# Hybrid decoder layer, first block: when the feed-forward weights are rounded, where a low half is made, and the order of loads around the output projection

## Chip, cores and metric

The kernel runs on one core of a Trainium2 chip. The metric is the device time of one execution in microseconds (us). The kernel before took 2597.31 us (median of three runs, 2594.66 to 2601.35).

## What is computed

One layer of a decoder on a prompt (2048 rows of 1024) and on a small sample group (8 x 4 rows): RMSNorm, one combined input projection, dilated windowed attention in 8 heads beside a spatial gating unit, one output projection with a residual add, RMSNorm, a SwiGLU feed-forward (width 2816) with a residual add, a last RMSNorm. The caches are written out as well. All arrays are float32. The change concerns the end of the layer:

```python
    x = x + jnp.concatenate([att, u * gate], axis=-1) @ w_out
    x = x + _swiglu(x, norm2_g, w_gate, w_up, w_down)
    ...
def _swiglu(x, g, w_gate, w_up, w_down):
    h = _rmsnorm(x, g)
    return (jax.nn.silu(h @ w_gate) * (h @ w_up)) @ w_down
```

## The kernel before

**Arithmetic.** TensorE (PE) multiplies operands that are cut into a rounded high half, made on ScalarE (ACT), and the rest, a low half, made by a subtraction on GpSimd (POOL) or VectorE (DVE). A product is then three matmuls: high x high, high x low, low x high. `split_sb` does both halves: high on ACT (L135), low on POOL or on the engine given as `eng_lo` (L138). The gate and up products of a slice of 128 feed-forward columns are formed by a scheme with seven products in place of eight (q = 0 to 6, each of 12 matmuls in L1663 to L1665), whose weight operands are sums of the loaded quarters.

**Blocks.** The 16 row tiles of 128 go through the output projection and the feed-forward in three blocks: six, six and four tiles. The change lies in the first block, from about 940 to 1495 us.

**Output projection, first block.** Each tile has an open half (columns 0 to 511) and a second half. The open half of tile 0 is multiplied during the attention. Then come the open halves of tiles 1 to 5 (24 matmuls each, L1411 to L1413), then the second halves of tiles 0 to 5. The input of a tile is loaded with `load_cat` (L1390) from the tensor `cat_d` in memory and split with `split_cat` (L1399 to L1403). `B.banks = (2, 0, 3, 4, 5, 2)`: tile 5's open half uses the PSUM bank of tile 0's, so it waits until `first_half(0)` has added tile 0's open half to `acc` (`open_end`, DVE, L1422). The weights of the second half are loaded by `half1_load` (L1363, into the eight buffers `fr`) and split by `half1_split`. In the same stretch `factors` loads the last head's softmax factors (`zn` and `raw` from `f_d`, L1077), and `rest` merges them on POOL (L1084 to L1088), stores the result (L1106) and loads the last gain. `sources` loads the first gate and up quarters into `fr` as they come free (L1560).

In the second phase `norm2_slot` runs between the tiles: it adds the second half (L1422), squares (L1450), forms the root and scales on ACT (L1462, `pair`), and PE transposes the result two tiles later (L1474). In the same steps the operands of slice 0 are formed: scaled on POOL (L1569), summed on DVE (L1584 to L1593).

**Feed-forward, first block.** Slices f = 0 to 21. Slice 0 is cut in two parts (four and two tiles). The operands of slice f + 1 are made during slice f, one stage per product, from the tables `ODD_STAGES` and `EVEN_STAGES`; the quarters of slice f + 2 are scaled on ACT (`gained`, L1572, eight operations of 128 columns per stage) and partly summed by the tables `..._AHEAD`. `sums` runs on POOL (L1584, L1587, L1590, and L1593 for operand 5, which overwrites operand 1); `both_halves` rounds on ACT (L1600) and makes the low half on POOL (L1604); `keep` stores an operand for the later blocks (`ab_d`, L1596). Product q = 0 is copied out of PSUM by ACT (L1673), and DVE adds the next products to that copy (L1675, L1677, L1687 and so on). The products use four PSUM banks in turn. `roll` copies 512 KB of cache from memory to memory (L1308). `w_down` is loaded into the one buffer `fd` (L1643) and split by `split_down` into `dw`, in even slices behind q = 6 and in odd ones behind q = 3. The down products of a pair of slices run in the even slice behind products 3, 4 and 5, two tiles each (L1743); they use two PSUM banks, which DVE frees by adding them to `acc` (L1745).

**What sets the order.** Each engine works through its own queue in order. DMAs are issued by SyncE (SP) in order as well. `tick()` counts a step per half unit or product, and `later(n, ...)` places work n steps on; inside a step the order of the calls is the order in the queues.

Of the kernel before, what the change touches and what calls it, by code (L numbers as in the profile page):

```python
# [23 lines left out]
KD = D // P  # L24
# [41 lines left out]
def hymba_step(ctx: ExitStack, tc: tile.TileContext, A: dict, O: dict):  # L66
    nc = tc.nc
    sync, act, dve, pool, pe = nc.sync, nc.scalar, nc.vector, nc.gpsimd, nc.tensor
# [633 lines left out]
    for half in range(2):  # L702
        for ki, kind in enumerate(ORDER[half]):
            for gi, tiles in enumerate(GROUPS):
# [13 lines left out]
                for j, tj in enumerate(tiles):  # L718
# [23 lines left out]
                    else:  # L742
                        layer_norm(e + 1, t, lambda t=t: zn["g", t], P)

                        f = e + 4 + (3 if tj in (4, 5) else 0)
# [526 lines left out]
    FC = 2  # L1272
# [333 lines left out]
    def both_halves(f, j):  # L1606
# [9 lines left out]
    ODD_STAGES = (((sums, 4), (sums, 3), (keep, 0)), ((sums, 1), (both_halves, 0), (keep, 6), (keep, 2)), ((both_halves, 1), (keep, 4)),  # L1616
                  ((both_halves, 2), (keep, 3)), ((both_halves, 3), (keep, 1)), ((sums, 5), (both_halves, 4)), ((both_halves, 5),),
                  ((both_halves, 6), (keep, 5)), ())
    EVEN_STAGES = (((both_halves, 0), (keep, 3)), ((both_halves, 1), (keep, 1)), ((both_halves, 2),), ((both_halves, 3),),
                   ((sums, 5), (both_halves, 4)), ((both_halves, 5),), ((both_halves, 6), (keep, 5)), (), ())  # L1620
    ODD_AHEAD = {5: ((gained, 0), (gained, 1)), 6: ((gained, 2), (gained, 3))}
    EVEN_AHEAD = {3: ((gained, 0), (gained, 1)), 4: ((gained, 2), (gained, 3), (keep, 0)), 5: ((sums, 4), (sums, 3), (keep, 6)),
                  6: ((sums, 1), (keep, 2), (keep, 4))}
# [20 lines left out]

    wd = {}

    def split_down(f):
        wd[f % FC] = ob_pair("dw")
        split_sb(*wd[f % FC], raws.pop(("d", f)))

    def product(B, u, q):

# [262 lines left out]
    def first_block(B):  # L1915

        for i in (1, 2):
            load_cat(B, i, 0, KD, acc_place(2 * i))
        plan.run(10 ** 9)
        split_cat(B, 1)  # L1920
        split_cat(B, 2)
        B.place()
        load_cat(B, 3, 0, KD)
        merge_store(h - 1, 2, 4)
        merge_store(h, 1, 2)
        load_acc(B, 1)
        load_acc(B, 0)
        half1_load(*range(4))
        load_cat(B, 4, 0, KD)

        def factors():
            for ch in (2, 3):
                merge_load(h, ch)
            load_cat(B, 5, 0, KD)
            half1_load(*range(4, KD))

        def rest():
            for ch in (2, 3):
                merge(h, ch, pool)
            merge_store(h, 2, 4)  # L1940
            sync.dma_start(gain[0], dap(A["final_g"], 0, [[0, P], [1, D]]))

        def first_half(i):
            open_end(B, i)
            norm2_half(B, i, B.X[0][:, i, 0:512])

        def root_ahead():
            t_ = fl.tile([P, 4], F32, name="s1", tag="s1", bufs=6)
            act.activation(t_[:, 0:1], ident[:, 0:1], AF.Sqrt)

        w = last_half["w"]
        for n, what in ((1, [(w.turn, lambda: ps_t(1)), (w.store, zn_tile)]), (2, [(split_cat, B, 3), (factors,)]),
                        (4, [(split_cat, B, 4), (rest,)]), (5, [(half1_split, B, dve, 0, 1)]),
                        (6, [(split_cat, B, 5), (first_half, 0)]), (7, [(first_half, 1), (half1_split, B, dve, 2, 3), (sources, B, 0, 0, 1, 2, 3)]),
                        (8, [(half1_split, B, None, 4, 5)]), (9, [(half1_split, B, dve, 6, 7)]),
                        (10, [(root_ahead,), (sources, B, 1, 0, 1, 2, 3), (first_operands, B)])):
            later(n, both, *what)
        for i in (1, 2):
            open_unit(B, i)
        for i in (3, 4, 5):  # L1960
            open_unit(B, i)

        def more_acc(i):
            if i in (1, 2):
                load_acc(B, 2 * i)
                load_acc(B, 2 * i + 1)

        second_phase(B, range(6), more_acc)
# [38 lines left out]
    for bi, B in enumerate(blocks):  # L2007
# [13 lines left out]
        def one(u, q):  # L2021
# [25 lines left out]
                roll(1)  # L2047

            if f % 2 == 0 and q == 6:
                split_down(f)  # L2050
                load_down(f + 1)
            elif f % 2 == 1 and q == 3:
                split_down(f)
                if f + 1 < NF:
                    load_down(f + 1)
# [143 lines left out]
```

## Time and profile before

| | |
|---|---|
| median of three runs | 2597.31 us |
| profiled execution, its own time | 2594.14 us |
| its span (first to last instruction) | 2592.3 us |
| mean granted clock of PE | 0.985 |
| PE busy | 2467.8 us (95%) |
| PE weight loads busy | 2175.4 us (84%) |
| DVE / ACT / POOL busy | 1430.4 / 1221.5 / 1369.7 us |

Times in the views are us from the start of the span. A row of the timeline has start, duration, engine, line, operation, output<-inputs, shapes, count, and in brackets how long the engine stood idle before it and who released it. A row of the list of waits has the waiting engine and line, the releaser, then the total in us, how often, and the longest. A row of the windows has the stretch, its length, for each of PE, PE's weight loads, DVE, ACT and POOL the busy time (and the number of instructions), then PE's granted clock, the DMA share and GB/s. A row of the chain has start, duration and what it is.

### The profile page before, as it was taken

To read this page: it belongs to the slowest core of one execution; us is meant where nothing else is said; L and a number is where in the kernel's file an instruction comes from. 1 tells how busy PE (TensorE), PEld (TensorE's weight loads), DVE (VectorE), ACT (ScalarE), POOL (GpSimd) and SP (SyncE) were. 2 spreads that over 40 slices of the span, in tenths; PEclk is the share of its full clock that TensorE was granted. 3 is DMA by queue.
4 is the path that set the end of the run, shared out by engine and by line. 5 is a ranking of instruction groups with operands and counts; after the bars stand their busy time and mean duration, and the time that the engine had idled before them with its cause. 6 is when DMAs were issued, how large, how long until landed. Compare 5 with 4: busy or idle time off the path is not lost.

```text
span 2592.3 us, 38968 instructions
## 1 busy us (share of the span) xinstructions
PE 2467.8 (95%) x13598; PEld 2175.4 (84%) x13598; DVE 1430.4 (55%) x2783; ACT 1221.5 (47%) x2578; POOL 1369.7 (53%) x1068
## 2 busy tenths in 40 slices
PE   8998899999999889999999999999999999999996
PEld 6777776677988768898999988999999987999996
DVE  3359686345888877344444466544444457544445
ACT  5423335446878745554454545432332336444332
POOL 2035654123576745776776743554453634766662
PEclk9999999999999999999999999999999999999998
DMA  7764853588678674464564564455463643755553
GB/s 236 226 204 150 272 159 117 180 247 276 195 223 219 175 210 150 143 206 156 163 195 134 183 187 159 171 187 175 151 215 126 210 154 127 239 194 196 195 195 109
DMA packets 313409, 480.00 MB, mean 185 GB/s; under 512 B 25841, under 2 KB 178834, under 8 KB 307326
## 3 DMA queue, kind: packets, MB, share of 16 engines
q1 hardware_dynamic: 307740, 468.48, 56.7%
q10 hardware_dynamic: 5474, 9.04, 1.3%
q8 instruction: 108, 1.77, 0.3%
q14 instruction: 87, 0.71, 0.1%
HBM read 381.72 MB, written 165.83 MB: 211 GB/s over the span
## 4 chain that ended last, share of the span: by engine, by line
PE 36%; issue 8%; POOL 8%; DMA 4%; ACT 2%; DVE 2%; SPq 1%; POOLq 0%; ACTq 0%; DVEq 0%
PE ps_o L1743 12%; PE ps_m L1665 8%; PE ps_m L1663 8%; PE ps_m L1664 8%; POOL op L1604 2%; DMA ab_d<-pair 2%; ACT fr L1572 1%; POOL pair L1584 1%; POOL dw L138 1%; POOL fr L1587 1%; POOL pair L1593 1%; POOL pair L1590 1%; DMA out_yp_dram<-acc 1%; SPq L1390 1%; PE ps_o L1411 0%
## 5 line engine op out<-in xcount | busy, mean ns | idle before, releaser
L1604 POOL TENSOR_TENSOR op<-fr,op 128x512 fp32r<-128x512 f32 x385 | 488.6, 1298 | 285.1 <-ACT op L1600 273.9
L1665 PE MATMUL ps_m<-xh,op 128*128 128x384 f32 (+5 forms) x1932 | 610.8, 316 | 2.0 <-POOL op L1604 2.0
L1663 PE MATMUL ps_m<-xh,op 128*128 128x384 f32 (+5 forms) x1932 | 610.9, 316 | 0.0
L1664 PE MATMUL ps_m<-xl,op 128*128 128x384 f32 (+5 forms) x1932 | 609.8, 316 | 0.0
L1743 PE MATMUL ps_o<-dw,hw 128*128 128x512 f32 x2040 | 485.8, 393 | 14.8 <-DVE acc L1745 14.8
L1743 PEld LDWEIGHTS ps_o<-dw,hw 128*128 128x128 f32 x2040 | 380.5, 188 | 98.4 <-DVE acc L1745 21.9
L1663 PEld LDWEIGHTS ps_m<-xh,op 128*128 128x128 f32 x1932 | 364.2, 189 | 4.0
L1664 PEld LDWEIGHTS ps_m<-xl,op 128*128 128x128 f32 x1932 | 364.2, 189 | 3.5
L1665 PEld LDWEIGHTS ps_m<-xh,op 128*128 128x128 f32 x1932 | 364.1, 188 | 2.5 <-POOL op L1604 2.5
L1745 DVE TENSOR_TENSOR acc<-acc,ps_o 128x512 f32<-128x512 f32 (+1 forms) x362 | 247.1, 687 | 214.8 <-PE ps_o L1743 214.7
L1710 ACT ACTIVATE ps_t<-zn 128x384 f32<-128x384 f32 (+1 forms) x126 | 58.2, 462 | 463.9 <-DVE zn L1693 364.5
L1600 ACT ACTIVATE op<-fr 128x512 fp32r<-128x512 f32 x396 | 235.5, 623 | 20.8 <-DMA fr<-ab_d 18.1
L138 POOL TENSOR_TENSOR dw<-fd,dw 128x1024 fp32r<-128x1024 f32 x66 | 158.5, 2402 | 120.1 <-ACT dw L135 119.4
L318 PE MATMUL ps_s<-wh,xh 128*128 128x512 f32 x480 | 197.2, 411 | 6.1 <-ACT xh L135 6.0
L319 PE MATMUL ps_s<-wl,xh 128*128 128x512 f32 x480 | 191.7, 399 | 2.0 <-DVE wl L226 2.0
L320 PE MATMUL ps_s<-wh,xl 128*128 128x512 f32 x480 | 191.5, 399 | 0.0
L1604 POOL TENSOR_TENSOR op<-pair,op 128x512 fp32r<-128x512 f32 x63 | 81.2, 1297 | 117.1 <-ACT op L1600 117.1
L1720 ACT ACTIVATE hw<-ps_t 128x384 fp32r<-128x384 f32 (+1 forms) x126 | 56.1, 453 | 175.1 <-DVE ps_t L1716 174.1
L318 PEld LDWEIGHTS ps_s<-wh,xh 128*128 128x128 f32 x480 | 92.5, 193 | 35.9 <-issue 8.4
L319 PEld LDWEIGHTS ps_s<-wl,xh 128*128 128x128 f32 x480 | 92.8, 193 | 20.8 <-DVE wl L226 3.6
L320 PEld LDWEIGHTS ps_s<-wh,xl 128*128 128x128 f32 x480 | 92.2, 192 | 20.4 <-DVE xl L138 0.2
L135 ACT ACTIVATE dw<-fd 128x1024 fp32r<-128x1024 f32 x66 | 69.8, 1057 | 73.1 <-DMA fd<-in_w_down_dram 73.1
(489 smaller groups left out, 4769.6 us busy)
## 6 DMA issues: line engine op xcount, KB each, us to landing
fr<-ab_d SPq DMA_DIRECT2D x308, 256.0 KB
fd<-in_w_down_dram SPq DMA_DIRECT2D x66, 512.0 KB
out_ks_dram<-in_cache_k_dram SPq DMA_DIRECT2D x56, 512.0 KB
out_vs_dram<-in_cache_v_dram SPq DMA_DIRECT2D x56, 512.0 KB
ab_d<-fr SPq DMA_DIRECT2D x88, 256.0 KB
raw<-in_w_in_dram SPq DMA_DIRECT2D x72, 256.0 KB
qk_d<-pair SPq DMA_DIRECT2D x64, 256.0 KB
ab_d<-pair SPq DMA_DIRECT2D x63, 256.0 KB
```

Source lines behind the costliest of these rows:

```text
L135: act.activation(hi, src, AF.Copy)
L138: (eng_lo or pool).tensor_sub(lo, src, hi.bitcast(F32))
L318: pe.matmul(o[j], xh[:, k, :], wh, start=(k == 0), stop=False)
L319: pe.matmul(o[j], xh[:, k, :], wl, start=False, stop=False)
L320: pe.matmul(o[j], xl[:, k, :], wh, start=False, stop=(k == KD - 1))
L1600: act.activation(ops[f, j][0], ab[f][j], AF.Copy)
L1604: (pool if f or j in POOL_LOW else dve).tensor_sub(lo_, ab[f][j], hi.bitcast(F32))
L1663: pe.matmul(out, wh[:, ks], xh[:, :, k], start=(k == 0), stop=False)
L1664: pe.matmul(out, wh[:, ks], xl[:, :, k], start=False, stop=False)
L1665: pe.matmul(out, wl[:, ks], xh[:, :, k], start=False, stop=(k == 3))
L1743: pe.matmul(ps[0:nr], l_, r_[:, cs], start=(z == 0 and y == 0), stop=(z == FC - 1 and y == len(pairs) - 1))
L1745: dve.tensor_add(B.acc[i][0:nr, cs], B.acc[i][0:nr, cs], ps[0:nr])
```

## The change

Four edits, all in the first block:

- `EVEN_STAGES`: an empty stage comes first, so each operand of an even slice from 2 on is rounded one product later; operand 6 is now rounded in its own slice, at q = 0. Sum 5 and the stores move with their stages.
- `split_down` of slice 0 makes the low half on DVE instead of POOL.
- The inputs of tiles 4 and 5 are loaded ahead of the first weights of the second half; tile 5's no longer inside `factors`. Of the `acc` loads, tile 0's comes first.
- `first_half(0)` runs one step earlier, ahead of the split of tile 5, and both ahead of the split of the first two weights of the second half, which comes one step later.

```diff
-    EVEN_STAGES = (((both_halves, 0), (keep, 3)), ((both_halves, 1), (keep, 1)), ((both_halves, 2),), ((both_halves, 3),),
-                   ((sums, 5), (both_halves, 4)), ((both_halves, 5),), ((both_halves, 6), (keep, 5)), (), ())
+    EVEN_STAGES = ((), ((both_halves, 0), (keep, 3)), ((both_halves, 1), (keep, 1)), ((both_halves, 2),), ((both_halves, 3),),
+                   ((sums, 5), (both_halves, 4)), ((both_halves, 5),), ((both_halves, 6), (keep, 5)), ())
...
-    def split_down(f):
+    def split_down(f, eng_lo=None):
         wd[f % FC] = ob_pair("dw")
-        split_sb(*wd[f % FC], raws.pop(("d", f)))
+        split_sb(*wd[f % FC], raws.pop(("d", f)), eng_lo=eng_lo)
...
         merge_store(h, 1, 2)
+        load_acc(B, 0)
+        load_cat(B, 4, 0, KD)
         load_acc(B, 1)
-        load_acc(B, 0)
+        load_cat(B, 5, 0, KD)
         half1_load(*range(4))
-        load_cat(B, 4, 0, KD)

         def factors():
             for ch in (2, 3):
                 merge_load(h, ch)
-            load_cat(B, 5, 0, KD)
             half1_load(*range(4, KD))
...
-                        (4, [(split_cat, B, 4), (rest,)]), (5, [(half1_split, B, dve, 0, 1)]),
-                        (6, [(split_cat, B, 5), (first_half, 0)]), (7, [(first_half, 1), (half1_split, B, dve, 2, 3), (sources, B, 0, 0, 1, 2, 3)]),
+                        (4, [(split_cat, B, 4), (rest,)]), (5, [(first_half, 0), (split_cat, B, 5)]),
+                        (6, [(half1_split, B, dve, 0, 1)]), (7, [(first_half, 1), (half1_split, B, dve, 2, 3), (sources, B, 0, 0, 1, 2, 3)]),
...
             if f % 2 == 0 and q == 6:
-                split_down(f)
+                split_down(f, dve if bi == 0 and f == 0 else None)
```

How the queues change, at the places that the prediction speaks of.

SP at the start of the first block, before: `cat_d<-ob` ahead of this are the stores of merged heads; `acc` is a residual tile, `fr<-in_w_out_dram` a weight of the second half (x4: four in a row), `xl` and `xh` the two parts of a tile's input, `zn` and `raw` from `f_d` the factors.

```order
L1352 DMA acc_9927<-in_x_prompt_dram 128x1024
L1352 DMA acc_9929<-in_x_prompt_dram 128x1024
L1363 DMA fr<-in_w_out_dram 128x512 x4
L1390 DMA xl_9920<-cat_d 128x8x128
L1390 DMA xh_9919<-cat_d 128x4x128
L1077 DMA zn<-f_d 128x512 x2
L1077 DMA raw<-f_d 128x512
L1077 DMA zn<-f_d 128x512
L1390 DMA xl_9920<-cat_d 128x8x128
L1390 DMA xh_9919<-cat_d 128x4x128
L1363 DMA fr<-in_w_out_dram 128x512 x4
```

The same place now:

```order
L1352 DMA acc_9927<-in_x_prompt_dram 128x1024
L1390 DMA xl_9920<-cat_d 128x8x128
L1390 DMA xh_9919<-cat_d 128x4x128
L1352 DMA acc_9931<-in_x_prompt_dram 128x1024
L1390 DMA xl_9920<-cat_d 128x8x128
L1390 DMA xh_9919<-cat_d 128x4x128
L1363 DMA fr<-in_w_out_dram 128x512 x4
L1077 DMA zn<-f_d 128x512 x2
L1077 DMA raw<-f_d 128x512
L1077 DMA zn<-f_d 128x512
L1363 DMA fr<-in_w_out_dram 128x512 x4
```

Both tiles' inputs moved ahead of four weights and the factors; the factors now have tile 5's input (768 KB) ahead of them that stood behind.

DVE in slice 1's first products, now (before, the row of `dw` was not there):

```order
L1716 TENSOR_TENSOR zn<-zn 128x128
L138 TENSOR_TENSOR dw<-fd,dw 128x1024
L1324 TENSOR_TENSOR hw<-zn,hw 128x2x64 x2
L1675 TENSOR_TENSOR raw<-zn,ps_m_10902 128x384
L1677 TENSOR_TENSOR zn<-zn,ps_m_10922 128x384
```

The low half of slice 0's `dw` now stands ahead of the adds that free slice 1's product banks.

ACT in an odd slice, from product 2 to the first products of the even slice behind it, before (`op` are rounded operands, from `fr` or `pair`; L1710 is the SiLU, L1720 rounds the hidden values):

```order
L1600 ACTIVATE op<-fr 128x512 x2
L135 ACTIVATE dw<-fd 128x1024
L1600 ACTIVATE op<-pair 128x512
L1710 ACTIVATE ps_t_11005<-zn 128x384
L1600 ACTIVATE op<-pair 128x512
L1572 ACTIVATE fr<-fr,g2c 128x128 x8
L1720 ACTIVATE hw<-ps_t_11005 128x6x64
L1720 ACTIVATE hw<-ps_t_10940 128x6x64
L1600 ACTIVATE op<-fr 128x512
L1572 ACTIVATE fr<-fr,g2c 128x128 x8
L1673 ACTIVATE zn<-ps_m_11051 128x384
L1600 ACTIVATE op<-fr 128x512
```

The same place now:

```order
L1600 ACTIVATE op<-fr 128x512
L135 ACTIVATE dw<-fd 128x1024
L1600 ACTIVATE op<-fr 128x512
L1710 ACTIVATE ps_t_11001<-zn 128x384
L1600 ACTIVATE op<-pair 128x512
L1572 ACTIVATE fr<-fr,g2c 128x128 x8
L1720 ACTIVATE hw<-ps_t_11001 128x6x64
L1720 ACTIVATE hw<-ps_t_10936 128x6x64
L1600 ACTIVATE op<-pair 128x512
L1572 ACTIVATE fr<-fr,g2c 128x128 x8
L1673 ACTIVATE zn<-ps_m_11047 128x384
L1600 ACTIVATE op<-fr 128x512 x2
```

Operand 5 (the second `op<-pair`) moved behind the first eight scalings and the hidden values, operand 6 behind L1673.

## Prediction

> **What bounds the kernel now.** I read the list of PE's waits between 920 and 1500 us first, since the edits lie there (first block of six tiles).
>
> ```profile
> PE ps_o L1743 <- DVE acc L1745: 10.8, 10, 3.0
> PE ps_m L1411 <- DVE acc L1422: 5.3, 1, 5.3
> PE ps_t L1474 <- ACT pair L1462: 3.0, 2, 2.3
> PE ps_m L1665 <- POOL op L1604: 2.0, 1, 2.0
> ```
>
> So a change of order can win about 21 us, plus what follows a wait. Next the timeline of PE at these waits, and the table by windows (its last three columns: granted clock, DMA share, GB/s).
>
> ```profile
> 968.68 0.76 PE L1411 MATMUL ps_m<-op,xh 128*128 128x512 f32 x1 [5.31 <-DVE acc L1422]
> 1054.20 0.44 PE L1665 MATMUL ps_m<-xh,op 128*128 128x384 f32 x1 [2.04 <-POOL op L1604]
> 1072.07 1.21 PE L1743 MATMUL ps_o<-dw,hw 128*128 128x512 f32 x3 [3.00 <-DVE acc L1745]
> 1120.38 0.96 PE L1743 MATMUL ps_o<-dw,hw 128*128 128x512 f32 x3 [0.81 <-DVE acc L1745]
> 1167.11 1.20 PE L1743 MATMUL ps_o<-dw,hw 128*128 128x512 f32 x4 [0.80 <-DVE acc L1745]
> ```
>
> ```profile
> 972.00:974.00 2.00, 2.00 (x7) 1.56 (x6) 1.41 (x2) 1.98 (x3) 2.00 (x2) 0.59 0.48 131
> 1042.00:1066.00 24.00, 21.96 (x118) 21.64 (x117) 8.12 (x14) 12.63 (x31) 22.61 (x17) 0.93 0.58 195
> 1066.00:1089.00 23.00, 20.00 (x86) 16.43 (x85) 10.28 (x17) 12.12 (x35) 12.31 (x10) 0.93 0.51 164
> 1112.00:1136.00 24.00, 23.19 (x114) 20.32 (x113) 10.39 (x18) 14.44 (x42) 14.15 (x12) 1.00 0.56 185
> ```
>
> After the waits of 5.31, 2.04 (at 1054) and 3.0 us (at 1072) the clock is granted by half: a mean of 0.59 says until about 973.6, so 4.9 us of work after the first wait (2.4 us lost); 0.93 of 23 to 24 us is 3.4 us at half after each of the others (1.7 us lost each). After a wait of 0.8 us it stays at 1.00. The Trainium skill ("TensorE: Matmul & The Clock Gate", What's actually happening) says that the gate watches a free-running window of about 3.4 us and halves the clock after an idle one. The trace agrees in kind, but 2.04 us idle sufficed here; by the page a new 1.7 us wait would cost nothing more, by the rows it may draw another 1.7 us.
>
> What one pair of slices costs without waits is read from the chain in block 1, whose six tiles do the same work:
>
> ```profile
> 1707.75 5.48 PE ps_o L1743 x24
> 1753.39 5.48 PE ps_o L1743 x24
> ```
>
> That is 45.64 us a pair; block 0 needs 46.73 (1120.38 to 1167.11), with a wait of 0.80 us and so 0.29 us for the restart.
>
> **Part 1, the even slices (term E).** Why does the first down product of a pair wait? Timeline of ACT, POOL and DVE ahead of the wait at 1120.38:
>
> ```profile
> 1109.73 1.29 POOL L1593 TENSOR_TENSOR pair<-fr,pair 128x512 f32<-128x512 f32 x1
> 1111.05 0.63 ACT L1600 ACTIVATE op<-pair 128x512 fp32r<-128x512 f32 x1 [3.52 <-POOL pair L1593]
> 1111.59 2.44 ACT L1572 ACTIVATE fr<-fr,g2c 128x128 f32<-128x128 f32 x8
> 1115.19 2.45 ACT L1572 ACTIVATE fr<-fr,g2c 128x128 f32<-128x128 f32 x8
> 1117.54 0.48 ACT L1673 ACTIVATE zn<-ps_m 128x384 f32<-128x384 f32 x1
> 1118.05 0.56 DVE L1675 TENSOR_TENSOR raw<-zn,ps_m 128x384 f32<-128x384 f32 x1 [2.59 <-ACT zn L1673]
> 1119.65 1.28 DVE L1745 TENSOR_TENSOR acc<-acc,ps_o 128x512 f32<-128x512 f32 x2
> ```
>
> ACT stands 3.52 us at the rounding of operand 5 (it needs sum 5 from POOL); behind it in the queue are both groups of eight scalings (2.44 us each) and the copy of the next slice's first product (L1673). DVE waits for that copy, so its adds L1745 come too late to free a bank. In the new order the first eight scalings stand ahead of operand 5, and operand 6 behind L1673. Then, with the wait for sum 5 running beside the scalings, the copy starts at sum 5's start + 1.3 + 0.6 + 2.44 + 0.05 = 4.4 us behind it, against 1117.54 - 1109.73 = 7.8 us now.
>
> What is added: the DMA that keeps operand 1 (sum 5 overwrites it) now stands behind one of operand 3 and a 512 KB roll.
>
> ```profile
> 1197.72 5.93 DMA ab_d<-pair
> ```
>
> It goes out behind the roll and so has 512 KB more ahead: at 303 KB/us (below) 1.7 us. In a pair near 1200 its landing set sum 5 (the row, from the chain: 5.93 us in flight); in the pair above POOL's L1593 names no DMA, so there is some slack. So sum 5 starts 0 to 1.7 us later and the copy 1.7 to 3.4 us earlier. PE needs L1745 only 0.8 us earlier. The wait goes; next late would be sum 5 itself. Operand 6 is rounded in its own slice's first step, six products (12 us) ahead of its use; POOL's queue only swaps the low half of `dw` with that of operand 3, so the busy time there is the same. By the first list ten pairs wait 10.8 us, the first of them 3.0; the other nine are counted here: 7.8 us of waits and 9 x 0.29 of restarts, **-10.4 us**; bounds -2 (sum 5 so late that a fifth is left of it) to -10.4.
>
> **Part 2, slice 0's `dw` on DVE, and the first pair (term D).** Timeline of POOL, DVE and PE:
>
> ```profile
> 1050.54 2.39 POOL L138 TENSOR_TENSOR dw<-fd,dw 128x1024 fp32r<-128x1024 f32 x1
> 1061.42 1.29 POOL L1593 TENSOR_TENSOR pair<-fr,pair 128x512 f32<-128x512 f32 x1
> 1044.17 2.69 DVE L1324 TENSOR_TENSOR hw<-zn,hw 128x128 fp32r<-128x128 f32 x2
> 1046.79 0.54 DVE L1675 TENSOR_TENSOR raw<-zn,ps_m 128x384 f32<-128x384 f32 x1
> 1045.03 1.04 ACT L135 ACTIVATE dw<-fd 128x1024 fp32r<-128x1024 f32 x1
> 970.46 1.29 DVE L138 TENSOR_TENSOR wol<-fr,wol 128x512 fp32r<-128x512 f32 x2 [1.32 <-ACT wol L135]
> 1049.57 0.33 PE L1663 MATMUL ps_m<-xh,op 128*128 128x384 f32 x1
> ```
>
> The low half of operand 6 runs right behind `dw` on POOL; without the 2.39 us it is there in time and the wait at 1054.20 goes. But on DVE `dw` must wait for ACT until 1046.07, and behind it stand the two L1324 and L1675, which frees the bank that the product at 1049.57 reuses (four banks in turn; slack 1049.57 - 1047.33 = 2.2 us). No row shows `dw` on DVE; two L138 of half its width took 1.29 us there (sixth row) while POOL stood, so `dw` about 1.3 alone. Beside a busy POOL two L1324 of 128 columns took 2.69 us, one POOL operation each. So `dw` ends between 1047.4 and 1048.7, the two L1324 between 1047.8 and 1051.4, L1675 0.5 us later, where 1049.57 is wanted: a new wait of 0 to 2.3 us. I take 1.7, since POOL is busy there. The Trainium skill ("SBUF — State Buffer", SBUF: two separate sides) speaks against this edit: the port pair that the two engines share is held for a whole instruction. With it the wait is the 1.7 us, without it about 0.
>
> Then the first pair. Its wait of 3.0 us at 1072.07 has the cause of term E, with POOL running without a gap from 1044: sum 5 came at 1061.42. POOL loses 2.4 us and is held up some 1.3 us by DVE, so sum 5 comes at about 1060.3 and ends at 1061.6; then operand 5 (0.6), scalings (2.44, perhaps 0.3 for their loads), copy and three DVE adds (2.1 us, as in 1117.54 to 1119.65), and one L1745 (0.69): PE goes on at about 1067.7 instead of 1072.07, without the half clock behind it (1.7 us). Whether PE got there at 1063.4 or 1065 does not matter then. **-5.6 us** with 0.4 for a half clock left over; bounds -9.0 (both waits, their restarts and half clocks) to -2 (the new wait at its longest, with a half clock). The next load of `fd`, which SP issues behind this `dw`, comes earlier, so nothing waits for it.
>
> **Part 3, the first open half and the loads (term A).** Timeline of DVE, ACT, POOL, SP:
>
> ```profile
> 955.61 0.63 ACT L1402 ACTIVATE xh<-xl 128x512 fp32r<-128x512 f32 x1 [9.24 <-DMA xl<-cat_d]
> 961.52 0.63 ACT L1402 ACTIVATE xh<-xl 128x512 fp32r<-128x512 f32 x1 [2.59 <-DMA xl<-cat_d]
> 967.87 0.67 DVE L1422 TENSOR_TENSOR acc<-acc,ps_m 128x512 f32<-128x512 f32 x1
> 957.25 1.73 POOL L1084 TENSOR_TENSOR ob<-ob,zn 128x512 f32<-128x512 f32 x1 [24.14 <-DMA zn<-f_d]
> 969.27 0.92 SPq L1560 DMA_DIRECT2D fr<-in_w_gate_dram  x1
> 975.53 2.04 POOL L1569 TENSOR_TENSOR fr<-fr,g2c 128x512 f32<-128x512 f32 x2 [0.93 <-DMA fr<-in_w_gate_dram]
> 977.61 1.51 DVE L1584 TENSOR_TENSOR raw<-fr 128x512 f32<-128x512 f32 x1 [2.46 <-POOL fr L1569]
> 982.21 0.69 DVE L1422 TENSOR_TENSOR acc<-acc,ps_o 128x512 f32<-128x512 f32 x1 [3.09 <-PE ps_o L1413]
> 985.42 1.16 ACT L1462 ACTIVATE pair<-acc,s 128x1024 f32<-128x1024 f32 x1 [1.04 <-DVE s L146]
> 987.45 1.03 PE L1474 MATMUL ps_t<-ident,pair 128*128 128x128 f32 x8
> ```
>
> Between the two landings (955.61, 961.52) the queue moved tile 4's `xh` (256 KB), four factor loads (1024) and tile 5's `xl` (512): 1792 KB in 5.91 us, 303 KB/us. Tile 4 has 1536 KB less ahead (one `acc`, four weights): 5.1 us earlier, if SP does not stand at it for the two stores issued at 941 to 944 that it reads; I allow 1 us, for which all loads behind it stand too. Tile 5 has 2048 KB less: 6.8 us earlier, at about 955. A split and one L1422 take 6.4 us now (961.52 to 968.5, POOL beside them), less with POOL idle until 960. So L1422 of tile 0 runs by 957 and tile 5 is split by 961, both ahead of 963.4, where PE wants the bank. The 5.31 us go, and 2.4 us of half clock: PE begins the second half at about 968.9 instead of 976.6. The first two weights' low halves come one step later, behind that split, and have until then, some 8 us. Those on POOL end near 972 (behind merges that end 2 us later), where PE wants them; at most 0.5 us.
>
> But the factors now have 768 KB more ahead: +2.5 us, so the merges on POOL, SP's stores behind them, the gate loads in SP's queue, L1569 and L1584 come about 2.0 us later (POOL shares its port with less DVE work), L1584 ending at 981.1. In DVE's queue the first L1422 of the second half stands behind it: 981.1 instead of 982.21. Its chain to L1462 ends 1.1 us earlier (985.5), and PE, there at 979.7, **waits about 5.8 us**, with the half clock behind it. Later tiles hang on this chain (the 2.3 us wait for L1462), not on PE. I take **-1.4 us**; bounds -7.7 (chain not late) to +1.5 (factors 2 us later still).
>
> **Rivals.** The second half isn't held and DVE doesn't hold up POOL (1.3 us more in D): A gives -7.7 and D -6.9, so 2572.3. Against it: the rows of L1569 and L1584, and DVE's 2.69 us for two small operations. A and D give nothing (the wait moves to L1474 and to the product at 1049.57, each with its half clock): 2587. E mostly doesn't come (sum 5 waits for the landing by 3 us): 2597.3 - 1.4 - 5.6 - 0.3 = 2590. On the other side, slower: sum 5 waits for its keep so long that ACT's queue holds up the copy more than now. The copy comes at sum 5's start + 4.4; it must start 3.4 us later than now to lose as much as today, and 5 us later to lose 2.3 us a pair plus 1.7 us of half clock: ten pairs at 4.0 instead of 1.09, +29 - 7 = 2619. The 5.93 us row is for it; that the burst in front grows by one roll only is against. That the order does not change as said is excluded by the listing of the queues.
>
> **How the numbers follow.** On the profiled execution (2594.1 us, span 2592.3): -10.4 - 5.6 - 1.4 = -17.4, so 2576.7. The median of the runs is 2597.3, 3.2 above; from it 2579.9, which I predict as 2580. Forecast 0.60; not held 0.10; A and D nothing 0.12; E missing 0.12; slower 0.06. A measurement of this kernel tells about 0.3% (7.8 us) from no change: faster 0.82, same 0.12, slower 0.06. The range reaches from a little under the second case to a little over the fourth: 2570 to 2591; less than 1 in 10 is left out above it, and a few in 100 below.
>
> **What would show it.** Right: no wait of L1743 for L1745 from the second pair on, pairs of 45.7 us; no wait of L1411; a wait of 4 to 6 us of L1474 for L1462 near 980; a wait of a product for L1675 near slice 1's sixth product. Wrong: L1593 released by a DMA in most pairs with L1743 still waiting; L1474 not waiting.

## The result and the profile after

The changed kernel takes 2577.43 us (median of four runs, 2575.45 to 2582.31) against 2597.26 us for the kernel before; the ratio is 0.9925, interval 0.9906 to 0.9944. Predicted were 2580 us (2570 to 2591).

The two profiled executions do not stand at the same time when the first block begins. The last transposition of attention weights (PE, L1057) is a good mark, since nothing ahead of it differs. From PE's timeline: this row, slice 0's first product (L1663) and the first down product of the last pair. First of before, then of after:

```profile
941.11 0.27 PE L1057 MATMUL ps_t<-ident,w 128*16 128x128 f32 x1
1018.76 0.36 PE L1663 MATMUL ps_m<-xh,op 128*128 128x256 f32 x1
1491.16 0.63 PE L1743 MATMUL ps_o<-dw,hw 128*128 128x512 f32 x2
```

```profile
946.68 0.27 PE L1057 MATMUL ps_t<-ident,w 128*16 128x128 f32 x1
1023.85 0.36 PE L1663 MATMUL ps_m<-xh,op 128*128 128x256 f32 x1
1481.36 0.63 PE L1743 MATMUL ps_o<-dw,hw 128*128 128x512 f32 x2
```

The mark is 5.57 us later in the profiled execution of after, so all its later times are read with 5.57 taken off: the first product comes 0.5 us earlier, the last pair 15.4 us earlier. PE's waits from 940 to 1500 us, after:

```profile
PE ps_t L1474 <- ACT pair L1462: 7.4, 3, 4.7
PE ps_o L1743 <- DVE acc L1745: 1.2, 2, 0.7
PE ps_m L1663 <- DVE raw L1675: 1.1, 1, 1.1
PE ps_o L1411 <- ACT wol L135: 0.6, 1, 0.6
```

Of ten waits of L1743 (10.8 us) two are left, and the waits of L1411 for L1422 and of L1665 for POOL are gone. In their place stand 4.4 us more at L1474, 1.1 us at L1663 and 0.9 us for the second-half weights (0.6 at L1411, 0.3 at L1412). Where most of them lie:

```profile
979.33 0.49 PE L1411 MATMUL ps_o<-wol,pair 128*128 128x512 f32 x1 [0.61 <-ACT wol L135]
991.67 1.97 PE L1474 MATMUL ps_t<-ident,pair 128*128 128x128 f32 x8 [4.70 <-ACT pair L1462]
1055.90 0.44 PE L1663 MATMUL ps_m<-xh,op 128*128 128x384 f32 x1 [1.09 <-DVE raw L1675]
1072.14 3.02 PE L1743 MATMUL ps_o<-dw,hw 128*128 128x512 f32 x12 [0.72 <-DVE acc L1745]
1255.47 0.50 PE L1743 MATMUL ps_o<-dw,hw 128*128 128x512 f32 x1 [0.47 <-DVE acc L1745]
```

**The second half** now begins 7.9 us earlier, and PE then stands at the first transposition. The chain that it waits for, from SP, POOL, DVE and ACT:

```profile
974.67 1.09 SPq L1106 DMA_DIRECT2D cat_d<-ob  x2
976.52 0.93 SPq L1560 DMA_DIRECT2D fr<-in_w_gate_dram  x1
983.76 4.48 POOL L1569 TENSOR_TENSOR fr<-fr,g2c 128x512 f32<-128x512 f32 x4 [5.84 <-DMA fr<-in_w_gate_dram]
985.84 1.51 DVE L1584 TENSOR_TENSOR raw<-fr 128x512 f32<-128x512 f32 x1 [5.18 <-POOL fr L1569]
990.47 1.15 ACT L1462 ACTIVATE pair<-acc,s 128x1024 f32<-128x1024 f32 x1 [1.04 <-DVE s L146]
```

The store goes out as the merges end (POOL, 974.64), the gate loads behind it, and L1569 waits 5.84 us for them; DVE stands at L1584, and the add, the root and the scale of tile 0 come behind. In the kernel before, L1569 began at 975.53, 34.4 us behind the mark; now it is 37.1. Behind the 4.70 us the clock is halved (granted 0.57 in this row of the windows):

```profile
990.00:998.00 8.00, 6.33 (x20) 5.39 (x21) 6.25 (x18) 5.10 (x10) 2.51 (x2) 0.57 0.86 304
```

**The pairs.** POOL, ACT and DVE ahead of a pair that now has no wait, and PE's first down product of it and of the next:

```profile
1109.60 1.29 POOL L1593 TENSOR_TENSOR pair<-fr,pair 128x512 f32<-128x512 f32 x1 [1.04 <-DMA ab_d<-pair]
1111.46 2.44 ACT L1572 ACTIVATE fr<-fr,g2c 128x128 f32<-128x128 f32 x8
1113.81 0.47 ACT L1673 ACTIVATE zn<-ps_m 128x384 f32<-128x384 f32 x1
1114.31 0.55 DVE L1675 TENSOR_TENSOR raw<-zn,ps_m 128x384 f32<-128x384 f32 x1 [3.95 <-ACT zn L1673]
1115.16 0.63 PE L1743 MATMUL ps_o<-dw,hw 128*128 128x512 f32 x2
1160.80 0.63 PE L1743 MATMUL ps_o<-dw,hw 128*128 128x512 f32 x2
```

The pair lasts 45.64 us. The copy L1673 starts 4.21 us behind sum 5 (7.81 before). But sum 5 itself now waits for the landing of its keep (1.04 us here; 0.2 to 2.5 us in each pair but the first). Where sum 5 came latest, at f = 10, PE still waited 0.47 us (1255.47), and that pair took 46.41 us.

### The profile page after: what moved, and what is told of

It is laid out like the page before. It is cut to its first block, busy times and chain, and to the rows that moved or that the text cites. A ratio compares the mean times of both kernels' runs of the same rounds, so it can differ in the third digit from the quotient of the medians.

```text
span 2580.5 us, 38980 instructions
## 1 busy us (share of the span) xinstructions
PE 2467.3 (96%) x13598; PEld 2178.8 (84%) x13598; DVE 1427.8 (55%) x2784; ACT 1221.9 (47%) x2578; POOL 1366.4 (53%) x1067
## 5 line engine op out<-in xcount | busy, mean ns | idle before, releaser
L1663 PE MATMUL ps_m<-xh,op 128*128 128x384 f32 (+5 forms) x1932 | 610.3, 316 | 1.1 <-DVE raw L1675 1.1
L1665 PE MATMUL ps_m<-xh,op 128*128 128x384 f32 (+5 forms) x1932 | 610.0, 316 | 0.0
L1743 PE MATMUL ps_o<-dw,hw 128*128 128x512 f32 x2040 | 482.0, 391 | 5.1 <-DVE acc L1745 5.1
L1743 PEld LDWEIGHTS ps_o<-dw,hw 128*128 128x128 f32 x2040 | 380.0, 188 | 85.5 <-DVE acc L1745 9.3
L1663 PEld LDWEIGHTS ps_m<-xh,op 128*128 128x128 f32 x1932 | 363.8, 188 | 5.5 <-DVE raw L1675 1.4
L1665 PEld LDWEIGHTS ps_m<-xh,op 128*128 128x128 f32 x1932 | 363.6, 188 | 0.0
L1710 ACT ACTIVATE ps_t<-zn 128x384 f32<-128x384 f32 (+1 forms) x126 | 58.3, 463 | 443.4 <-DVE zn L1693 336.7
L1720 ACT ACTIVATE hw<-ps_t 128x384 fp32r<-128x384 f32 (+1 forms) x126 | 56.1, 453 | 175.1 <-DVE ps_t L1716 174.2
L611 POOL TENSOR_TENSOR vl<-kv,vh 100x512 fp32r<-100x512 f32 (+1 forms) x32 | 46.0, 1439 | 110.3 <-ACT vh L605 35.2
```

Source lines behind the costliest of these rows:

```text
L1663: pe.matmul(out, wh[:, ks], xh[:, :, k], start=(k == 0), stop=False)
L1665: pe.matmul(out, wl[:, ks], xh[:, :, k], start=False, stop=(k == 3))
L1710: act.activation(g, c, AF.Silu)
L1743: pe.matmul(ps[0:nr], l_, r_[:, cs], start=(z == 0 and y == 0), stop=(z == FC - 1 and y == len(pairs) - 1))
```

## Experiments

Theory: three terms that hardly touch. The pairs gain because operand 5 and operand 6 leave the stretch of ACT's queue between sum 5 and the copy (E); the first pair gains with POOL's earlier sum 5 (D); the earlier second half gains nothing, since it hangs on merge, store, gate load, L1569, L1584 (A). Rivals are named with each run. The table gives, for all runs, the place of four rows of PE against the kernel before in us (minus is earlier), each counted from its own L1057, and the ratio of times with its interval.

| kernel | second half | slice 0's first product | first down product, f = 4 | same, f = 20 | ratio of times |
|---|---|---|---|---|---|
| after | -7.9 | -0.5 | -7.1 | -15.4 | 0.9925 (0.9906 to 0.9944) |
| after_again | -7.9 | +0.5 | -6.0 | -15.4 | 0.9922 (0.9905 to 0.9939) |
| e1_even_only | +0.7 | -0.2 | -2.9 | -12.3 | 0.9942 (0.9928 to 0.9956) |
| e2_loads_only | -7.9 | +0.5 | -1.1 | -0.9 | 0.9998 (0.9990 to 1.0007) |
| e3_dw_only | +0.4 | -0.4 | -1.9 | -2.1 | 0.9996 (0.9987 to 1.0004) |
| e4_gates_ahead_of_store | -7.9 | -3.6 | -10.2 | -19.2 | 0.9917 (0.9904 to 0.9931) |
| e5_keep1_late | -7.9 | +0.4 | -0.8 | +13.0 | 1.0040 (1.0020 to 1.0059) |
| e6_lows_ahead_of_dw | -7.9 | -0.6 | -7.1 | -16.5 | 0.9926 (0.9907 to 0.9945) |
| e7_sum5_on_pool | -7.9 | -4.1 | -10.7 | -19.5 | 0.9915 (0.9898 to 0.9931) |
| e8_factors_first | -7.9 | -1.7 | -8.2 | -17.6 | 0.9929 (0.9914 to 0.9944) |
| e9_operand6_only | +0.5 | +0.4 | 0.0 | -2.7 | 0.9970 (0.9960 to 0.9981) |
| e10_all | -7.9 | -7.7 | -14.0 | -22.7 | 0.9891 (0.9871 to 0.9911) |
| e11_keep1_early | -7.9 | -0.5 | -7.0 | -16.4 | 0.9925 (0.9906 to 0.9944) |

Runs e1 to e4 shared a chip, on which the kernel before took 2594.0 us; e5 to e8 (2593.35) and e9 to after_again (2594.14) another. The two traces of the changed kernel itself differ by 1.0 us at the first product (the merges begin 1.0 us later in after_again), so a difference of about 1 us in the middle columns tells nothing by itself.

### The three parts, each alone

`e1_even_only` is the kernel before with the new `EVEN_STAGES` and nothing else.

> Of the whole change only the empty first stage of EVEN_STAGES. Theory (the copy L1673 stood behind the rounding of operand 5, so behind sum 5, and now does not): pairs of 45.6 to 45.7 us against 46.73, nine waits of L1743 for L1745 gone, which is -9.3 to -10.4 us; the first pair's wait of 3.0 us shrinks by about 3 although POOL still makes the low half of dw, since the copy follows sum 5 by 4.4 us in place of 7.8: another -3 to -4.7 with its half clock. In all -12 to -15, so 2582 to 2585 us; the waits of 5.3 us (L1411) and 2.0 us (L1665) stay as they were. Rival (sum 5, which now waits for the landing of its keep, takes the gain back): pairs over 46.2, time 2590 or more. Rival (the gain of the pairs hangs on the earlier start of POOL given by the dw edit): first pair still waits 3 us, -9 at most.

2578.22 us, pairs of 45.64 us, no wait of L1743 but in the first pair. PE there, and POOL and ACT ahead of it:

```profile
1060.04 1.29 POOL L1593 TENSOR_TENSOR pair<-fr,pair 128x512 f32<-128x512 f32 x1 [0.39 <-DMA ab_d<-pair]
1064.24 0.47 ACT L1673 ACTIVATE zn<-ps_m 128x384 f32<-128x384 f32 x1
1067.07 0.50 PE L1743 MATMUL ps_o<-dw,hw 128*128 128x512 f32 x1 [2.07 <-DVE acc L1745]
```

The copy again comes 4.20 us behind sum 5. The gain is 15.0 us by the ratio (11.4 to 18.7), 12.3 in the trace at f = 20, as the theory has it; the rivals (2590 us, or 9 us at most) fall. The first pair, though, shrank only from 3.0 to 2.07 us, since sum 5 came later there (121.0 us behind the mark L1057; before 120.3).

`e2_loads_only` has only the loads and the earlier first open half.

> Of the whole change only the order of the loads and the earlier first open half. Theory (the second half hangs on the chain merge, store, gate load, scaling L1569, sum L1584, add L1422, scaling L1462, and not on PE): the wait of 5.3 us of L1411 goes, but a wait of 4 to 6 us of L1474 for L1462 takes its place, slice 1's first product comes 0 to 1.5 us earlier, time 2595.5 to 2597 us. Rival (the second half follows PE): no wait of L1474 over 2.5 us, first product 7 us earlier, 2589.6 us.

2593.17 us, no change (-2.6 to +1.8 us by the interval). The waits of PE:

```profile
PE ps_o L1743 <- DVE acc L1745: 10.9, 10, 3.0
PE ps_t L1474 <- ACT pair L1462: 7.8, 3, 5.1
```

The longest wait of L1474 is 5.1 us where 4 to 6 was expected; the first product is not earlier. The rival (2589.6 us) falls. That PE is 1.1 us earlier at f = 4 is the clock: behind the waits of 2.05 (L1665) and 3.00 us (L1743) no half clock came in this trace, where the kernel before had one behind each.

`e3_dw_only` has only slice 0's `dw` on DVE.

> Of the whole change only the low half of slice 0's dw on DVE. Theory: the wait of 2.04 us of L1665 for POOL goes with the half clock behind it (-3.7), a wait of about 1.1 us of a product for L1675 comes (+1.1 to +1.4); sum 5 comes 1 us earlier, and the first pair's wait of 3.0 us shrinks only by that much, since its copy still stands behind operand 5: -1. In all -3 to -4, so 2593 to 2594.5 us. Rival (the new wait takes its place, half clock included): 2597 us. Rival (the first pair's wait hung on POOL's dw alone): the 3.0 us go, -7 or more.

2592.26 us, -1.0 us by the ratio (-3.4 to +1.0); in the trace -1.9 at f = 4, less than the 3 to 4 us that I expected. The new wait is there:

```profile
PE ps_m L1663 <- DVE raw L1675: 1.1, 1, 1.1
```

The time cannot tell the theory from no change. In the trace no half clock stands behind the new wait, as the first rival needs, and the first pair waits 2.97 us as before, against the second rival: PE (2.9 us) and sum 5 (1.8 us) both came earlier, and PE waited another 0.83 us for ACT's hidden values (L1720). So neither e1 nor e3 alone frees the first pair. Together they do (0.72 us in after), and without a half clock, which both single runs still had there: after stands 6.6 us better from slice 0's first product to f = 4, e1 2.7, e3 1.5. Of the 2.4 us that e1 and e3 lack, 1.7 is that half clock (3.41 us in each of them). By f = 20 the three runs sum to 15.3 us against 15.4, in part by chance: e2's 0.9 us is the clock, and after lost 1.1 us at f = 10 and 12.

### What the second half hangs on

`e4_gates_ahead_of_store`, on the changed kernel:

```diff
                 merge(h, ch, pool)
-            merge_store(h, 2, 4)
-            sync.dma_start(gain[0], dap(A["final_g"], 0, [[0, P], [1, D]]))
...
-                         ... (half1_split, B, dve, 2, 3), (sources, B, 0, 0, 1, 2, 3)]),
+                         ... (half1_split, B, dve, 2, 3), (sources, B, 0, 0, 1, 2, 3), (rest_out,)]),
```

where `rest_out` holds the two removed lines.

> The changed kernel, with the first four gate and up loads ahead of the store of the last merged head and of the last gain in SP's queue (they stood behind). Theory (the second half is held by the chain merge, store, gate load, scaling, sum, add): the gate loads go out near 966 to 972 in place of 976.5, L1569 runs right behind the split of the second-half weights near 978 in place of 983.8, L1584 ends 5 to 6 us earlier, and the wait of 4.7 us of L1474 with the half clock behind it (3.4 us) is gone or under 1 us: -5 to -8 us against the changed kernel's 2577.4, so 2569.5 to 2572.5 us. Rival (the chain add, square, root, scale of each tile sets the pace whatever the loads do): the wait comes back at the next tiles, 2575 us or more.

2572.08 us. POOL's scaling, PE at the first transposition, then DVE and PE at tile 3:

```profile
972.90 4.93 POOL L1569 TENSOR_TENSOR fr<-fr,g2c 128x512 f32<-128x512 f32 x4
983.95 0.27 PE L1474 MATMUL ps_t<-ident,pair 128*128 128x128 f32 x1
```

```profile
996.89 0.97 DVE L1593 TENSOR_TENSOR raw<-fr,raw 128x512 f32<-128x512 f32 x1
997.79 1.77 DVE L1604 TENSOR_TENSOR op<-fr,op 128x512 fp32r<-128x512 f32 x1
999.49 0.68 DVE L1422 TENSOR_TENSOR acc<-acc,ps_m 128x512 f32<-128x512 f32 x1
1006.45 0.47 PE L1474 MATMUL ps_t<-ident,pair 128*128 128x128 f32 x1 [2.25 <-ACT pair L1462]
```

L1569 comes 31.8 us behind the mark in place of 37.1 and waits for no load; the 4.70 us are gone. So the cause is shown: it was the place of the gate loads behind the store (and behind the load of the last gain, which e4 moves with it). The gain is smaller than expected, 3.1 us at the first product (by the ratios 1 to 2 us, which their intervals cannot tell from nothing), and a part of what the rival says came true, a wait at a later tile: tile 3's add stands behind slice 0's own sum 5 and low half in DVE's queue and PE waits 2.25 us there, with the clock halved behind it, and once more behind three waits for the second-half weights (the last at 975.54, 1.6 us in all).

`e8_factors_first` is the changed kernel with `half1_load(*range(4))` behind the factor loads in place of ahead of them.

> The changed kernel, with the factor loads ahead of the first four weights of the second half (1024 KB), and no other edit: the store still stands ahead of the gate loads. Theory (second half held by the chain merge, store, gate load): the factors land 3.4 us earlier (1024 KB at 303 KB/us), the merges end 3.4 us earlier, so the store, the splits of the last four weights, the gate loads, L1569 and L1584 too; the wait of 4.7 us of L1474 falls to about 1.3 us, the waits of 0.6 and 0.3 us for the weights go; slice 0's first product comes 3 to 5 us earlier, of which tiles 3 and 4 give back some 2: 2573 to 2575 us. Rival (L1569 waits for the gate loads' buffers or bandwidth and not for the store): the wait of L1474 stays over 3.5 us, 2577 us.

2575.30 us. POOL and PE:

```profile
978.49 4.48 POOL L1569 TENSOR_TENSOR fr<-fr,g2c 128x512 f32<-128x512 f32 x4 [5.73 <-DMA fr<-in_w_gate_dram]
986.40 0.47 PE L1474 MATMUL ps_t<-ident,pair 128*128 128x128 f32 x1 [4.88 <-ACT pair L1462]
```

A miss: the wait was to fall to 1.3 us. Against after, the merges began only 2.0 us earlier and took 1.0 us longer (DVE worked beside them), so L1569 came 0.9 us earlier, and PE, which waited only 0.3 us for weights, came earlier too. The first product moved by 1.2 us. These are differences that after and after_again have as well (L1569 at 37.1 and 38.4 us behind the mark), so this run by itself decides nothing; the rival's reason for the wait (buffers or bandwidth, not the store) is excluded by e4.

`e7_sum5_on_pool` is e4 with slice 0's sum 5 and its low half 3 on POOL.

> The kernel with the gate loads ahead of the store, and besides that, in the first block, slice 0's sum 5 and the low half of its operand 3 on POOL in place of DVE. Theory (with the gate loads early, what holds tiles 3 and 4 of the second half is slice 0's own operand work, which stands in DVE's queue ahead of the L1422 of tile 3): that L1422 comes 2.5 us earlier, the wait of 2.25 us of L1474 falls under 0.5 us, its half clock with it; -2 to -4 us against the kernel with the gate loads ahead, so 2568 to 2570 us on its chip. Rival (the chain of each tile on ACT sets the pace): the wait stays over 1.5 us, 2571 us or more.

2572.22 us; beside e4 no gain that can be told. The expected fall of the wait under 0.5 us did not come; the figures are those of the rival (over 1.5 us, 2571 us or more). ACT:

```profile
1003.20 0.63 ACT L1600 ACTIVATE op<-raw 128x512 fp32r<-128x512 f32 x1 [1.02 <-POOL raw L1593]
1005.40 0.63 ACT L1450 ACTIVATE xh<-acc 128x512 fp32r<-128x512 f32 x1
```

DVE's L1422 of tile 3 now runs as the tile ends, but ACT stands at the rounding of operand 5, which waits for POOL's sum 5, and tile 3's square (L1450) is behind it. The wait moved from DVE's queue to ACT's; L1474 still waits 1.61 us.

`e10_all` takes e4 and e7 and adds three edits:

```diff
-            for ch in (2, 3):
-                merge(h, ch, pool)
+            merge(h, 2, pool)
...
+                         ... (half1_split, B, dve, 2, 3), (merge, h, 3, dve), (sources, B, 0, 0, 1, 2, 3),
...
-                    ((sums, 5), (low_half, 3), (low_half, 4), (high, 5)), ((high, 6), (low_half, 5), (keep, 5)), ((low_half, 6),))
+                    ((sums, 5), (low_half, 3), (low_half, 4)), ((high, 6), (high, 5), (keep, 5)), ((low_half, 5), (low_half, 6)))
```

and the edit of e6 (below).

> The changed kernel with what the earlier runs point to, all in the first block: gate loads ahead of the store; slice 0's sum 5 and low half 3 on POOL, and now operand 5 rounded a stage later (it stood in ACT's queue ahead of tile 3's squares and waited for POOL); the merge of the last chunk on DVE, which stood 8 us there, in place of POOL; the low half of slice 0's dw behind the two small L1324. Theory: the merges end 2 to 2.5 us earlier, so the waits of 1.6 us for the second-half weights and the half clock behind them go; the wait of 1.6 us of L1474 for tile 3 goes; slice 0's first product comes 4 to 5 us earlier than in the kernel with the gate loads ahead alone, 7 to 9 us earlier than in the changed kernel: 2568 to 2570.5 us, about 7 us under the changed kernel on the same chip. Rival (the second half is by now paced by each tile's own chain of add, square, root and scale): under 3 us gained, 2573 us or more.

2564.86 us (2563.85 to 2572.08), 10.0 us under the changed kernel on the same chip (2572.96 to 2575.92, no overlap), the fastest of all. The traces show 7.4 us of this at f = 20; where the rest lies is not shown. PE's waits, and the row of the windows with the clock:

```profile
PE ps_t L1474 <- ACT pair L1462: 2.5, 3, 1.1
PE ps_o L1743 <- DVE acc L1745: 1.6, 2, 1.2
PE ps_o L1412 <- DVE wol L138: 1.3, 2, 0.8
```

```profile
940.00:1130.00 190.00, 184.44 (x998) 165.09 (x997) 103.98 (x204) 105.14 (x242) 120.43 (x91) 1.00 0.57 184
```

The first product is 4.1 us earlier than in e4. Some 3.4 us of that is clock: no wait is longer than 1.22 us, and the clock is full from 940 to 1130 (0.98 in e4). The merges ended 1.3 us earlier, less than expected, and 1.3 us of waits for the weights stay.

### The first pair

`e6_lows_ahead_of_dw` changes the order of three operations on DVE, on the changed kernel: slice 0's `dw` behind the two small L1324, by

```diff
-                split_down(f, dve if bi == 0 and f == 0 else None)
-                load_down(f + 1)
+                    act.activation(hi, src, AF.Copy)
+                    later(1, dve.tensor_sub, lo_, src, hi.bitcast(F32))
+                    later(1, load_down, 1)
```

for the first slice (its `dw` then carries the line of the step counter, L1324).

> The changed kernel, with the low half of slice 0's dw behind the two small L1324 in DVE's queue in place of ahead of them (and the next load of fd behind that). Theory (the wait of 1.09 us of the product for L1675 is the place in the queue: DVE stood 1.85 us for ACT's dw while the L1324 could have run): dw ends 1 to 1.5 us earlier, the wait goes, sum 5 of the first pair comes no later, so the first pair gains 0 to 1.1 us; time 2576 to 2577.5 us. Rival (the shared time of DVE and POOL: whatever order, the three operations take 4.3 us): the wait stays at 0.9 to 1.3 us.

2572.55 us. DVE and PE:

```profile
1039.34 2.68 DVE L1324 TENSOR_TENSOR hw<-zn,hw 128x128 fp32r<-128x128 f32 x2
1041.94 1.21 DVE L1324 TENSOR_TENSOR dw<-fd,dw 128x1024 fp32r<-128x1024 f32 x1
1043.08 0.54 DVE L1675 TENSOR_TENSOR raw<-zn,ps_m 128x384 f32<-128x384 f32 x1
1045.61 0.44 PE L1665 MATMUL ps_m<-xh,op 128*128 128x384 f32 x1 [0.35 <-POOL op L1604]
```

The wait of 1.09 us for L1675 is gone, as by the theory; a wait of 0.35 us for POOL takes a part of its place, and the first pair waits 1.17 us in place of 0.72. At f = 4 the kernel stands where after stood (-7.1): the gain was given back whole, since the first pair goes on when sum 5 lets it (118.4 us behind the mark in both), whenever PE gets there.

### The pairs: what stands between sum 5 and the copy

`e9_operand6_only` is the kernel before with operand 6 one stage later and operand 5 where it was:

```diff
-                   ((sums, 5), (both_halves, 4)), ((both_halves, 5),), ((both_halves, 6), (keep, 5)), (), ())
+                   ((sums, 5), (both_halves, 4)), ((both_halves, 5),), (), ((both_halves, 6), (keep, 5)), ())
```

> The kernel before, with only operand 6 of the even slices rounded one stage later (behind the copy L1673 in ACT's queue); operand 5 stays ahead of both groups of scalings. Theory (the copy comes at sum 5 + the sum of what stands between in ACT's queue): one rounding less between, 0.5 us, so the copy comes 7.3 us behind sum 5 in place of 7.8; the waits of L1743 shrink from 0.80 to about 0.3 us, pairs 46.1 to 46.3 us, nine pairs -4 to -6 us: 2588 to 2590 on a chip where the kernel before takes 2594. Rival (only the place of operand 5 behind the first scalings counts): waits stay at 0.8, pairs 46.7, no change. Rival (any earlier copy frees the bank): waits gone, pairs 45.7, -10 us.

2587.03 us, -7.8 us by the ratio (-4.9 to -10.4), a little more than expected; in the trace most pairs are of 46.2 us with a wait of 0.3 us, the one of f = 4 here:

```profile
1118.32 0.50 PE L1743 MATMUL ps_o<-dw,hw 128*128 128x512 f32 x1 [0.29 <-DVE acc L1745]
```

One rounding less between sum 5 and the copy takes 0.5 us off the wait. That is the queue's arithmetic; by the pairs both rivals (no change, waits gone) fall. The place of PE at f = 20 is only 2.7 us earlier, since at f = 8 and 10 sum 5 waited 1.0 and 0.8 us for its keep and the pairs took 47.27 and 47.13 us. The time gained some 5 us more than this, which is not explained.

`e5_keep1_late` is the changed kernel with `(keep, 1)` two stages later, in the stage of operand 3.

> The changed kernel, with the keep of operand 1 in the even slices two stages later (behind operand 3 in place of operand 1), so that sum 5, which overwrites operand 1, waits for that landing. Theory (the copy L1673 starts 4.2 to 4.4 us after sum 5 starts, and PE stands as soon as that is later than now before the change): sum 5 starts two products of an odd slice later (3.3 us), up to 5 with the further roll in front of the keep; so the copy comes 1 to 3 us later than before the change, the waits of L1743 for L1745 are back in all ten pairs with 1.9 to 3.6 us each, some with a half clock; pairs of 48 to 49.5 us, in all 20 to 40 us over the changed kernel, 2597 to 2617 us. Rival (POOL and ACT catch up, sum 5 has slack of several us): pairs under 46.2, less than 2583 us.

2602.38 us, slower than both kernels. POOL, ACT and PE at the second pair:

```profile
1108.03 1.29 POOL L1593 TENSOR_TENSOR pair<-fr,pair 128x512 f32<-128x512 f32 x1 [4.60 <-DMA ab_d<-pair]
1112.23 0.47 ACT L1673 ACTIVATE zn<-ps_m 128x384 f32<-128x384 f32 x1
1115.06 0.50 PE L1743 MATMUL ps_o<-dw,hw 128*128 128x512 f32 x1 [2.21 <-DVE acc L1745]
```

Sum 5 waits 4.60 us for the landing, the copy follows 4.20 us behind it, PE waits 2.2 us; pairs of 48.5 us. This is the slower rival of the prediction, brought about by an edit, and it works as that said. Its price was set too high there, 4.0 us a pair against 2.9 measured, by the half clocks: only two of the nine pairs from f = 4 on drew one.

`e11_keep1_early` has `(keep, 1)` in the empty first stage.

> The changed kernel, with the keep of operand 1 of the even slices in the first stage, which is empty in the changed kernel. Theory (sum 5's wait for that landing, 0.2 to 2.5 us in every pair, has cover of 1 to 2 us and costs only where it is longest): sum 5 is released by no DMA in most pairs and starts up to 1.5 us earlier, the copy too, yet pairs stay at 45.64 us; only the wait of 0.5 us in one or two pairs goes: 0 to -1 us against the changed kernel. Rival (the wait costs in every pair): pairs under 45.5 us, -2 us or more.

2575.82 us, the changed kernel's time. POOL in the third pair:

```profile
1150.83 1.29 POOL L1593 TENSOR_TENSOR pair<-fr,pair 128x512 f32<-128x512 f32 x1
```

Sum 5 waits for no DMA in any pair and every pair is of 45.64 us; the trace is 1.0 us better than that of after at f = 20, which the time can't tell. The run after_again, whose sums 5 wait 0.2 to 1.4 us for the keep, lost nothing in its pairs either. So the wait for the keep has cover, and costs only where sum 5 comes latest.

### The changed kernel again

> The changed kernel itself, as a measure beside the other three on the same chip: 0.990 to 0.994 of the kernel before. By the theory its own wait of 4.5 to 5 us of L1474 near 980 and its pairs of 45.64 us come back, while the place of the half clocks behind waits of about 2 us differs from run to run.

2574.89 us; its wait of L1474 is 5.04 us, the pairs 45.64 us, without the loss at f = 10.

## Why the prediction was right

**Term E, -10.4 us.** Right in cause and size. From f = 4 to f = 20, eight pairs, e1, e11 and after_again gain 9.4 us, and 10.5 with the ninth; the profiled execution of after gained 8.3 and 9.4, since f = 10 took 46.41 us and f = 12 45.96. The step "copy at sum 5's start + 4.4" measured 4.20 to 4.21 in three kernels. The bound on sum 5 (0 to 1.7 us later) held in six of nine pairs (from the first down product: -5.6 us at f = 4 against -6.9 before); in the others it came 1.8, 2.8 and 3.3 us later (f = 8, 12 and 10). The bound was thus too narrow; that it cost only about 1 us is owed to the 3.6 us that the copy had gained. Against what I had set down as a sign of being wrong, L1593 is released by a DMA in most pairs; but without L1743 waiting, so the sign as a whole did not come. From f = 4 on, in all traces, PE's wait is the place of the copy behind the first down product less 0.1 us (copy at +0.57: wait 0.47; at +2.30: 2.21; at -0.22: none; only the last one of e3, 1.15 us at +0.89, is longer).

**Term D, -5.6 us.** It measured -6.6 (after) and -6.5 (after_again). The mechanism was the one named, but the booking was not clean: e1 and e3 show that the first pair's gain belongs to neither edit alone. Part of the size is chance as well: the term counts a half clock of 1.7 us behind the 3.0 us wait, and e2 shows that this half clock does not always come. The step mis-sized is sum 5's start, 1.1 us earlier predicted, 1.9 measured (from the mark). The row of after:

```profile
1065.10 1.29 POOL L1593 TENSOR_TENSOR pair<-fr,pair 128x512 f32<-128x512 f32 x1
```

DVE held POOL up by 0.9 us, not 1.3, and the first product itself came 0.5 us earlier. The new wait was 1.09 us in place of 1.7. It did not matter, which e6 shows, as the prediction said.

**Term A, -1.4 us.** It measured -0.5 and +0.5, and e2 alone +0.5: nothing. The mechanism is shown by e4; the mis-sized step is the chain's delay, 2.0 us predicted. L1569 came 2.7 us later: the merges began 3.3 us later, not 2.5, and took 1.6 us less than in before, and from their end to L1569 it was 1.0 us more. SP issued the first factor load 4.1 us later (13.0 us behind the mark, before 8.9): it had stood 1.8 us at tile 4's load for the stores that this reads, where 1 us was allowed, and for the factors the prediction counted the 2.5 us of bytes alone. In after_again (14.1 us) L1569 came 4.0 us later. I also did not see that the splits of the last four weights wait for the merges' buffers and for the landing of the store (0.9 us of PE's time in after).

**The sum.** -17.4 was predicted on the trace; at the end of PE's work the traces of after and after_again show -17.9 and -18.0. This is closer than the terms deserve: 16.5 us of it lie in the first block and some 1.4 behind it, which no term holds, and in after the errors offset one another (D gave 1.0 us more, A 0.9 and E 1.0 us less). The medians differ by 19.8 (14.5 to 24.4). The 2 us more are not explained by the block; the profiled executions differ by more than that ahead of the mark (last section).

**The rivals.** "Second half not held" is excluded by the wait at L1474; "A and D give nothing" was true of A alone; "E missing" and "sum 5 waits for its keep" did not happen but for f = 10 and 12 in after (1.1 us), and e5 shows the second, with sum 5 5.0 us later than in before (-1.9 us against -6.9 from the first down product); at 4.20 us from sum 5 to the copy, the old loss comes back at 3.6 us (predicted 3.4).

## What to carry to other kernels

Count what stands in an engine's queue between the producer and the instruction that frees a bank: here one rounding taken out of that stretch gave back its 0.5 us per pair (e9), and moving the copy 3.6 us forward gave back what there was to gain, 1.09 us per pair (e1). An engine that starts earlier gains nothing if the next thing it needs hangs on a load that stands behind a store in the DMA queue; look for that load first, then for what is next late, since e4, e6 and e7 each moved a part of the wait, or nearly all of it, to the next queue. Keeping every wait short pays twice, by the wait and by the clock (e10).

## What the runs showed of the chip

**The clock behind a wait.** In the fourteen traces (before, after and twelve more), from 940 to 1500 us, none of 20 waits of PE of 1.0 to 1.7 us was followed by a half clock; of 28 waits of 2.0 to 3.0 us 12 were, for 3.41 us, the same wait in one trace and not in the next (2.25 us in e4 yes, 2.24 in e1 no; in the changed kernel itself 2.16 no and 2.20 yes); all of 12 waits from 4.4 us were, ten of them for 6.83 us. The Trainium skill ("TensorE: Matmul & The Clock Gate", What's actually happening) has a window that runs free of the work; the shares fit that, though waits well under its 3.4 us suffice. My 1.7 us for each wait over 2 us was thus right in less than half of them. Short waits in close order can count together: 1.6 us in three (972.99 to 975.54 in e4) drew a half clock; but 1.6 us in four (973.88 to 977.21 in e2) drew none, and 1.3 us in two (972.08 and 973.52 in e10) none.

**Starts that differ.** The mark L1057, with the same program ahead of it, came at 941.11 in before, 946.68 in after and at 935.23 us in e5. The clock goes with it: up to the mark PE ran at the half clock for 44 us in before, 61 in after and 34 in e5. A span alone can't tell a change of a few us here; places counted from a common row can.

**DVE beside POOL.** DVE in after, the same two subtractions beside POOL's merges and with POOL idle:

```profile
967.85 3.03 DVE L138 TENSOR_TENSOR wol<-fr,wol 128x512 fp32r<-128x512 f32 x2 [1.31 <-ACT wol L135]
979.36 1.29 DVE L138 TENSOR_TENSOR wol<-fr,wol 128x512 fp32r<-128x512 f32 x2 [8.48 <-ACT wol L135]
```

3.03 against 1.29 us. Two of 128x128, a quarter of the size, took 2.66 us in after and 2.68 in e6 beside POOL. What a DVE operation costs there depends on POOL's instruction more than on its own size; the Trainium skill's rule ("SBUF — State Buffer", SBUF: two separate sides) that the shared port pair is held for a whole instruction fits these rows. The one for `dw` (128x1024) took 1.63 us in after and 1.21 in e6, both beside POOL (whose L1587 took 2.15 and 2.35 us there, 1.29 alone), so where it falls against POOL's instruction matters too.
